# Scores, sums' transposes and the gate's sums emitted one to three ticks later in a hybrid backbone layer

## The chip, the cores and the metric

The kernel runs on one NeuronCore of a Trainium2 chip. The metric is the device time of one execution in microseconds; of several executions the median is taken. TensorE is called PE here (its weight loads PEld), VectorE DVE, ScalarE ACT, GpSimd POOL and SyncE SP.

## What is computed

One layer over 256 latent tokens and 256 context tokens, width 4096, all in float32:

```
mod_l = silu(c) @ w_ada + b_ada ;  mod_c = silu(c_ctx) @ w_ada + b_ada      # shift, scale, gate
hl = rmsnorm(xl) * (1 + sc_l) + sh_l ;  hc = rmsnorm(xc) * (1 + sc_c) + sh_c
zl = hl @ w_in ;  zc = hc @ w_in                                            # split in nine parts
ya = conformer_conv(a_val, a_glu)      # 31 taps depthwise, channel LayerNorm, swish, pointwise
yb = rg_lru forward + rg_lru backward  # short conv, two gates, one scan in each direction
yc = neighbourhood_attention(q, k, v, k_ctx, v_ctx, rpb)                    # 16 heads of 128
mix = concat(ya * silu(a_gate), yb * silu(r_gate), yc * silu(c_gate))
out = rmsnorm(xl + g_l * (mix @ w_out))
```

## The kernel before

The two big products, with `w_in` and `w_out`, are made on PE in chunks of 512 columns of weights. A chunk is cut into steps of at most two blocks of 128 rows (`kp`). For each step SP loads the raw weights (L433), ACT makes their rounded high part `hi` (L439), DVE the rest `lo` = raw - hi (L445), and `products` (L454) multiplies three times for each row block and PSUM bank: high by high, the two cross terms. A step of the later chunks has two banks, so twelve matmuls of 512 columns. `hi` and `lo` have three buffers each (`NHI`), `raw` has six (`NRAW`). During a step the program emits the `hi` and the `lo` of the step two places on.

Beside the products stand small programs written as generators ("threads"): `mod_finish` turns the sums of the modulation (`adas`) with PE transposes into columns (`psm`), `next_h`/`make_h` make the normalised input `h` from them, `attention` does four heads at a time (scores `sc` L681, softmax, transposes `pt` L706 of the probabilities `pr`, values `y`), `convs` does the 31 taps of eight channel blocks on DVE (L773, L777), `conv_ln` what follows them, and `finish` of a `GItem` sums the gate.

The gate's columns of `w_ada` are weighted and added up on DVE, 32 row blocks for each of four groups: the first block of a group starts the sum `gboth` anew (L1168), the others add to it (L1170). After the last, `finish` is spawned: eight one-column matmuls with `ones` (`psg`, L1187) sum over the partitions, and DVE adds the bias into `gcol` (L1189). The next group's first block overwrites `gboth`, so its `emit` first calls `drain` on that thread.

A tick is one group of three matmuls (of six in the chunks of the pointwise product); a step of two banks and two row blocks has four. After each group every thread that is due is advanced; `yield None` in a thread means "not before the next tick", `yield a, b` charges its time to DVE's and ACT's credit. A thread of rank 0 always goes on; the others go on only while the credit of their engine lasts. The order in which things are emitted is the order in each engine's queue. Two small functions set it, and `drain` has its own rule: it advances threads by force, without looking at the credit, and emits no products meanwhile.

```
while forced or clock[th.engine] > (clock["reserve"] if th.rank > 3 else 0):   # advance
    r = next(th.gen)                    # goes on until the thread yields None or ends
...
for t in list(threads):                                                        # drain
    if not t.done and (t in ts or t.rank == 0 or clock["aux"] > 0):
        advance(t, True)
clock["tick"] += 1
```

`clock["aux"]` counts the three small PSUM banks that are held (`take`, `give`). `convs` yields `0.5, 0` after each tap, and None only while it waits for its inputs.

Of the kernel before, what the change touches and what calls it, by code (L numbers as in the profile page):

```python
# [47 lines left out]
def tile_hybrid_layer(ctx: ExitStack, tc: tile.TileContext, x, c, cctx_tok, c_ctx, w_ada, b_ada,  # L48
# [10 lines left out]
    def page(shape, dt=F32, name="pg"):  # L59
        uid[0] += 1  # L60
        return pg.tile(shape, dt, name=f"{name}_{uid[0]}", tag="pg", bufs=NPG)
# [7 lines left out]
    def pair(name):  # L69

        if wides[0] < NWD:
            wides[0] += 1
            t = wide([P, 2, 512], name=name)
            return [t[:, 0], t[:, 1]], 1
        return [page([P, 512], name=name) for _ in range(2)], 0

    def unpair(p):
        wides[0] -= p[1]

    def bank(name, tag="aux"):  # L80


        uid[0] += 1
        return pp.tile([P, 512], F32, name=f"{name}_{uid[0]}", tag=tag, bufs=5 if tag == "g" else 3)

    def small(n, name):
        uid[0] += 1
        return sp.tile([P, n], F32, name=f"{name}_{uid[0]}", tag="small", bufs=8)
# [60 lines left out]
    def pause(n):  # L149
        for _ in range(n):  # L150
            yield None

    def take(n):

        while clock["aux"] + n > clock["limit"]:
            yield None
        clock["aux"] += n

    def give(n):
        clock["aux"] -= n  # L160

    with tc.manual_schedule():
# [49 lines left out]
        def col(name, i, n=1):  # L212
            gi, r = where[name]
            return cols[:, gi, r + i:r + i + n]
# [51 lines left out]
        def mod_columns(part, k0, s, sums):  # L266
            dst = (modG if part == 0 else modS)[:, k0:k0 + s, :]
            ba = col("b_ada", (KT if part == 0 else 0) + k0, s)[:, :, None].to_broadcast([P, s, 2])
            V.tensor_add(dst, sums[:, :s], ba)
            if part == 0:  # L270
                V.scalar_tensor_tensor(dst, dst, 1.0, col("norm_g", k0, s)[:, :, None].to_broadcast([P, s, 2]),
                                       ALU.add, ALU.mult)

        def mod_matmuls(ps, raw, k, n, W):
            for j in range(n):
                q = (k + j) % 4
                mm(ps[32 * q:32 * q + 32, :W], cpad[(k + j) // 16][:, (k + j) % 16, :], raw[:, j, :],  # L277
                   start=(k + j < 4), stop=(k + j >= KT - 4))

        def mod_finish(part, k0, s, ps):  # L280

            V.tensor_copy(adas[:, :s * P], ps[:, :s * P])
            give(1)
            yield 0.6 * s / 4 + .1, 0
            yield from pause(6)
            yield from take(1)
            pm = bank("psm")
            for i in range(s):
                tr(pm[:, i * P:(i + 1) * P], adas[:, i * P:(i + 1) * P], ident)
            yield None  # L290
            sums = small(8, "sums").rearrange("p (k o) -> p k o", o=2)
            V.reduce_sum(sums[:, :s], pm[:, :s * P].rearrange("p (k q o) -> p k o q", q=4, o=32)[:, :, 0:2], axis=AX.X)
            mod_columns(part, k0, s, sums)
            give(1)
            yield 0.5, 0
# [60 lines left out]
            V.tensor_scalar(t, t, -0.5, 1.5, ALU.mult, ALU.add)  # L356
            V.tensor_mul(y, y, t)

        for _ in range(7):
            next(fin0)  # L360
        rst = cp.tile([P, 4], F32, name="rst")
        V.reduce_sum(rst, ss, axis=AX.X)
# [273 lines left out]
        def turned(tm, i):  # L636

            ps = bank("turn")
            for j in range(2):
                for b in range(2):  # L640
                    tr(ps[:, j * T + b * P:j * T + b * P + P], tm[b][:, (i + j) * P:(i + j + 1) * P], ident)  # L641
            return ps
# [10 lines left out]
        def attention(g, st):  # L653
            qs = st["q"][0]
            yield from take(2)
            ps = [turned(qs, i) for i in (0, 2)]
            yield None
            for t, b in zip(qs, ps):
                A.copy(t.rearrange("p (r c) -> p r c", c=64)[:, :, ::-1], b.rearrange("p (r c) -> p r c", c=64))
                yield 0, 0.7  # L660
            give(2)
            q = [t[:, j * T:(j + 1) * T] for t in qs for j in range(2)]
            B, Ps = page([P, 384], name="B"), pair("pr")
            B3 = B.rearrange("p (a b) -> p a b", b=64)

            def bias(h):
                for rl in range(2):
                    G.dma_start(B3[64 * rl:64 * rl + 64],
                                bass.AP(tensor=rpb.tensor, offset=rpb.offset + h * 465 + (5 - rl) * 31 - 48,
                                        ap=[[1, 64], [31, 6], [1, 64]]))  # L670
                G.tensor_mul(B3, B3, mask[:, 0:1].to_broadcast([P, 6, 64]))
                G.tensor_add(B3, B3, mask[:, 1:2].to_broadcast([P, 6, 64]))

            for i in range(4):
                h = 4 * g + i
                bias(h)
                sums = []
                for qt in range(2):
                    yield from take(1)
                    ps = bank("sc")  # L680
                    mm(ps, q[i][:, qt * P:(qt + 1) * P], acc[("k", g), i], start=True, stop=True)  # L681
                    yield None
                    off = P * (1 - qt)
                    V.tensor_add(ps[:, T:], ps[:, T:], B[:, off:off + T])
                    nm, sm = small(1, "nm"), small(1, "sm")
                    V.reduce_max(nm, ps, axis=AX.X, negate=True)
                    yield 1.2, 0
                    A.activation(Ps[0][qt], ps, AF.Exp, bias=nm, accum_out=sm)
                    give(1)
                    yield 0, 0.7  # L690
                    sums.append(sm)
                yield None
                for qt in range(2):
                    V.reciprocal(sums[qt], sums[qt])
                    A.mul(Ps[0][qt], Ps[0][qt], sums[qt])  # L695
                    yield 0.2, 0.75
                yield None
                yield None
                yield None
                yield from take(2)  # L700
                pt = []
                for kp in range(2):
                    ps = bank("pt")
                    for kt in range(2):
                        for qt in range(2):
                            tr(ps[:, kt * T + qt * P:kt * T + qt * P + P],  # L706
                               Ps[0][qt][:, (2 * kp + kt) * P:(2 * kp + kt + 1) * P], ident)
                    pt.append(ps)
                yield None
                for kp in range(2):  # L710
                    A.copy(Ps[0][kp].rearrange("p (r c) -> p r c", c=64)[:, :, ::-1],
                           pt[kp].rearrange("p (r c) -> p r c", c=64))
                    give(1)
                    yield 0, 0.7
                yield None
                yield from take(1)
                ps = bank("y")
                for qt in range(2):
                    for kt in range(4):
                        v = acc[("v", g), kt] if kt < 2 else st["v"][0][kt - 2]  # L720
                        mm(ps[:, qt * P:(qt + 1) * P], Ps[0][kt // 2][:, (kt % 2) * T + qt * P:(kt % 2) * T + qt * P + P],  # L721
                           v[:, i * P:(i + 1) * P], start=(kt == 0 and qt == 0), stop=(kt == 3), skip_group_check=True)
                yield None
                for qt in range(2):
                    cg = st["cg"][0][qt][:, i * P:(i + 1) * P]
                    V.scalar_tensor_tensor(cg, cg, 0.5, ps[:, qt * P:(qt + 1) * P], ALU.mult, ALU.mult)
                give(1)
                yield 0.6, 0
                if i % 2:
                    yield None  # L730
                    yield from take(1)
                    ps = turned(st["cg"][0], i - 1)
                    yield None
                    split_mix([16 + h - 1, 16 + h], ps)
                    give(1)
                    yield 0.9, 0.8
            for t in (Ps, st["q"], st["v"], st["cg"]):
                unpair(t)
# [416 lines left out]
        class GItem:  # L1155
# [22 lines left out]
                return [self.emit]  # L1178

            def finish(self):  # L1180
                yield None
                yield None
                yield from take(1)
                pm = bank("psg")
                a = gboth.rearrange("p a b -> p (a b)")
                for j in range(8):
                    mm(pm[:, j:j + 1], a[:, j * P:(j + 1) * P], ones, start=True, stop=True)  # L1187
                yield None
                V.tensor_add(gcol[:, 8 * self.sg:8 * self.sg + 8], pm[:, 0:8], col("b_ada", 2 * KT + 8 * self.sg, 8))  # L1189
                give(1)  # L1190
                yield 0.1, 0
# [200 lines left out]
```

## Time and profile before

| | |
|---|---|
| median of 3 runs | 2342.5 us (2339.43 to 2342.91) |
| profiled execution, its own time | 2338.42 us |
| span from first to last instruction | 2336.6 us |
| mean granted clock of TensorE | 0.991 |
| PE busy | 2263.8 us (97%), 10761 matmuls |
| DVE, ACT busy | 1595.1 us (68%), 1251.5 us (54%) |
| read from HBM | 544.58 MB, 235 GB/s over the span |

PE is busy 97% of the span; every other engine is far below that. So the time is that of PE's queue plus PE's idle time, and a view of PE's waits says what the idle time hangs on. A matmul of 512 columns shows as 0.39 us long, but the next one starts 0.23 us after it; the starts give the pace.

### The profile page before, as it was taken

What the parts mean: (1) busy time and instruction counts of PE and PEld (TensorE: products, weight loads), DVE (VectorE), ACT (ScalarE), POOL (GpSimd) and SP (SyncE); (2) the same over time, 40 slices, a digit from 0 to 9 for tenths busy, and PEclk for the clock granted to TensorE, in tenths of its full rate; (3) what the DMA queues carried; (4) which work ended last, traced back from release to release, by engine and by line L of the source; (5) the groups of instructions that cost most, each with busy time, mean ns of one, the idle gap of its engine ahead of it and who ended that gap; (6) DMA issues with size and microseconds to landing.
All of it is one profiled execution on the core that took longest, in us unless ns stands there. A gap on an engine that the chain in (4) does not pass through costs nothing. (4 is left out here: it accounts for less than half of the span.)

```text
span 2336.6 us, 29786 instructions
## 1 busy us (share of the span) xinstructions
PE 2263.8 (97%) x10761; PEld 1748.7 (75%) x10761; DVE 1595.1 (68%) x2196; ACT 1251.5 (54%) x1846; POOL 90.6 (4%) x133
## 2 busy tenths in 40 slices
PE   6999999999999999999999999999999999999997
PEld 4556556677777888777777887888888779888886
DVE  5543477587776546676776897788777767667655
ACT  5665545465565768776754444544454544344443
POOL 0000000000000000000001000100010111000000
PEclk8999999999999999999999999999999999999999
DMA  9988888878877445555677887878887778787864
GB/s 314 290 264 281 307 270 299 293 259 258 263 258 261 132 116 156 170 171 159 168 205 212 273 283 219 225 242 261 233 217 237 184 226 306 261 266 253 262 213 162
DMA packets 293483, 550.76 MB, mean 236 GB/s; under 512 B 19199, under 2 KB 60887, under 8 KB 293335
## 3 DMA queue, kind: packets, MB, share of 16 engines
q1 hardware_dynamic: 287904, 536.94, 71.3%
q0 software_dynamic: 4480, 11.54, 4.4%
q8 instruction: 84, 1.38, 0.3%
q14 instruction: 64, 0.52, 0.1%
q10 hardware_dynamic: 951, 0.37, 0.1%
HBM read 544.58 MB, written 4.19 MB: 235 GB/s over the span
## 5 line engine op out<-in xcount | busy, mean ns | idle before, releaser
L445 DVE TENSOR_TENSOR lo<-raw,hi 128x1024 fp32r<-128x1024 f32 (+1 forms) x660 | 753.7, 1144 | 463.2 <-ACT hi L439 460.5
L439 ACT CAST hi<-raw 128x1024 fp32r<-128x1024 f32 (+1 forms) x660 | 647.4, 986 | 721.9 <-PE gtm L454 410.6
L454 PE MATMUL gtm<-hi,lh 128*128 128x512 f32 x2560 | 835.0, 401 | 1.7 <-ACT hi L439 1.7
L454 PEld LDWEIGHTS gtm<-hi,lh 128*128 128x128 f32 x2560 | 482.4, 188 | 112.5 <-issue 10.8
L454 PE MATMUL gtm<-lo,lh 128*128 128x512 f32 x1280 | 502.0, 392 | 6.4 <-DVE lo L445 6.2
L454 PE MATMUL gboth<-h,hi 128*128 128x512 f32 x1536 | 489.9, 400 | 9.1 <-ACT acc L887 3.3
L454 PEld LDWEIGHTS gboth<-h,hi 128*128 128x128 f32 x1536 | 280.3, 188 | 126.9 <-issue 52.5
L454 PE MATMUL gtm<-hi,mix 128*128 128x512 f32 x976 | 303.2, 390 | 0.0
L454 PE MATMUL gboth<-h,lo 128*128 128x512 f32 x768 | 301.2, 392 | 0.7 <-DVE lo L445 0.7
L454 PEld LDWEIGHTS gtm<-lo,lh 128*128 128x128 f32 x1280 | 241.2, 188 | 70.1 <-DVE lo L445 12.3
L454 PEld LDWEIGHTS gtm<-hi,mix 128*128 128x128 f32 x976 | 183.2, 188 | 37.9
L454 PE MATMUL gtm<-lo,mix 128*128 128x512 f32 x488 | 190.1, 390 | 0.2 <-DVE lo L445 0.2
L454 PE MATMUL gtm<-hi,h 128*128 128x512 f32 x512 | 177.7, 401 | 9.2 <-DVE acc L892 6.9
L967 DVE SCALAR_TENSOR_TENSOR gboth<-raw,scol,gboth 128x512 f32<-128x512 f32 x248 | 171.4, 746 | 0.3 <-DMA raw<-in_w_ada_dram 0.3
L454 PEld LDWEIGHTS gboth<-h,lo 128*128 128x128 f32 x768 | 144.7, 188 | 33.6 <-DVE lo L445 1.8
L887 ACT COPY acc<-gboth 128x512 f32<-128x512 f32 x216 | 123.7, 584 | 74.9 <-PE gboth L454 73.6
L1170 DVE SCALAR_TENSOR_TENSOR gboth<-raw,scol,gboth 128x1024 f32<-128x1024 f32 x124 | 160.8, 1297 | 0.0
L454 PEld LDWEIGHTS gtm<-hi,h 128*128 128x128 f32 x512 | 97.4, 190 | 43.4 <-DVE acc L892 10.0
L897 ACT COPY gboth<-acc 128x512 f32<-128x512 f32 x216 | 123.8, 591 | 8.9 <-DVE acc L892 7.2
L277 PE MATMUL psa<-raw,cpad 128*32 128x512 f32 (+2 forms) x1152 | 114.4, 470 | 1.6 <-DMA raw<-in_w_ada_dram 1.2
L454 PEld LDWEIGHTS gtm<-lo,mix 128*128 128x128 f32 x488 | 91.6, 188 | 19.5 <-DVE lo L445 0.8
L892 DVE TENSOR_TENSOR acc<-acc,gboth 128x512 f32<-128x512 f32 x72 | 49.3, 685 | 80.6 <-PE gboth L454 80.4
(227 smaller groups left out, 1673.1 us busy)
## 6 DMA issues: line engine op xcount, KB each, us to landing
raw<-in_w_in_dram SPq DMA_DIRECT2D x430, 512.0 KB, 4.5
raw<-in_w_ada_dram SPq DMA_DIRECT2D x384, 512.0 KB, 4.8
raw<-in_w_out_dram SPq DMA_DIRECT2D x128, 512.0 KB, 4.7
raw<-in_w_in_dram SPq DMA_DIRECT2D x100, 256.0 KB, 4.0
xp<-in_ctx_dram SPq DMA_DIRECT2D x16, 256.0 KB, 6.9
xp<-in_x_dram SPq DMA_DIRECT2D x16, 256.0 KB, 6.5
xr<-in_x_dram POOLq DMA_DIRECT2D x16, 256.0 KB, 5.1
raw<-in_w_pw_dram SPq DMA_DIRECT2D x8, 512.0 KB, 6.3
```

Of the source, the lines that this page charges most:

```text
L277: mm(ps[32 * q:32 * q + 32, :W], cpad[(k + j) // 16][:, (k + j) % 16, :], raw[:, j, :], start=(k + j < 4), stop=(k + j >= KT - 4))
L439: A.copy(self.hi[:, :n], self.raw[:, :n])
L445: V.tensor_sub(self.lo[:, :n], self.raw[:, :n], self.hi[:, :n].bitcast(F32))
L454: one = lambda o, l, r, start, stop: mm(o, l, r, start=start, stop=stop, skip_group_check=True)
L887: A.copy(acc[key, i], b)
L892: V.tensor_add(acc[key, i], acc[key, i], b)
L897: A.copy(ch.banks[i], acc[ch.name, i])
L967: V.scalar_tensor_tensor(a, self.raw[:, j], s, a, ALU.mult, ALU.add)
L1170: V.scalar_tensor_tensor(a, self.raw, s, a, ALU.mult, ALU.add)
```

## The change

Four places of the emission change. `mod_finish` pauses nine ticks between the copy of the sums and their transposes where it paused six, and holds a lock, `adas_busy`, from the copy to the transposes, so that a second `mod_finish` does not overwrite `adas`; the loop of the start that steps the first of these threads takes ten steps for seven. `attention` yields once more between the copies of the turned queries and the first scores. `finish` pauses five ticks before the gate's one-column matmuls where it paused two. Three `yield None` in `attention` become `pause(3)`, which is the same. No instruction is added or taken away.

```diff
+        adas_busy = []
+
         def mod_finish(part, k0, s, ps):
 
+            while adas_busy:
+                yield None
+            adas_busy.append(1)
             V.tensor_copy(adas[:, :s * P], ps[:, :s * P])
             give(1)
             yield 0.6 * s / 4 + .1, 0
-            yield from pause(6)
+            yield from pause(9)
             yield from take(1)
             pm = bank("psm")
             for i in range(s):
                 tr(pm[:, i * P:(i + 1) * P], adas[:, i * P:(i + 1) * P], ident)
+            adas_busy.clear()
             yield None
...
-        for _ in range(7):
+        for _ in range(10):
             next(fin0)
...
                 yield 0, 0.7
             give(2)
+            yield None
             q = [t[:, j * T:(j + 1) * T] for t in qs for j in range(2)]
...
-                yield None
-                yield None
-                yield None
+                yield from pause(3)
                 yield from take(2)
...
             def finish(self):
-                yield None
-                yield None
+                yield from pause(5)
                 yield from take(1)
                 pm = bank("psg")
```

The line numbers of the changed kernel are higher: L445 becomes L451, L454 L460, L289 L294, L777 L782, L1168 L1173, L1170 L1175, L1187 L1191, L1189 L1193.

Where the first gate group ends, DVE's queue before reads as follows (`gboth` is the sum, `gcol` its result, `lo` the low part of a step's weights, `conv` the taps):

```order
L777 SCALAR_TENSOR_TENSOR conv_10636<-conv_10636,cols 128x248
L1170 SCALAR_TENSOR_TENSOR gboth<-raw_11400,scol,gboth 128x1024
L445 TENSOR_TENSOR lo_11500<-raw_11402,hi_11491 128x1024
L1189 TENSOR_TENSOR gcol<-psg_11505,cols 128x8
L1168 TENSOR_SCALAR gboth<-raw_11423,scol 128x1024
L445 TENSOR_TENSOR lo_11529<-raw_11425,hi_11520 128x1024
L777 SCALAR_TENSOR_TENSOR conv_10636<-conv_10636,cols 128x249
```

Here two small operations stand between the low part of one step and that of the next. The same place of DVE's queue in the changed kernel, first and last rows:

```order
L1175 SCALAR_TENSOR_TENSOR gboth<-raw_11400,scol,gboth 128x1024
L451 TENSOR_TENSOR lo_11500<-raw_11402,hi_11491 128x1024
L782 SCALAR_TENSOR_TENSOR conv_10636<-conv_10636,cols 128x249
L782 SCALAR_TENSOR_TENSOR conv_10636<-conv_10636,cols 128x250
L782 SCALAR_TENSOR_TENSOR conv_10636<-conv_10636,cols 128x251
...
L782 SCALAR_TENSOR_TENSOR conv_10636<-conv_10637,cols,conv_10636 128x242
L782 SCALAR_TENSOR_TENSOR conv_10636<-conv_10637,cols,conv_10636 128x241
L1193 TENSOR_TENSOR gcol<-psg_11515,cols 128x8
L1173 TENSOR_SCALAR gboth<-raw_11423,scol 128x1024
L451 TENSOR_TENSOR lo_11582<-raw_11425,hi_11510 128x1024
```

Between the same two low parts now stand 53 operations of `convs` (52 taps and one L773, here L778), then the two of the gate.

PE's queue where the transposes of one modulation's sums stand (the place of about 459 us in the profile), before:

```order
L454 MATMUL gtm_3982<-hi_3947,h_715_3377 128x512
L289 MATMUL psm_4035<-ident,adas_91 128x128 x4
L454 MATMUL gtm_4042<-hi_3947,h_715_3377 128x512
L454 MATMUL gtm_4042<-lo_3962,h_715_3377 128x512
L454 MATMUL gtm_4042<-hi_3947,h_715_3377 128x512
L454 MATMUL gtm_3982<-hi_3984,h_721_3409 128x512
```

The transposes `psm` follow the first group of a step. In the changed kernel PE's queue there reads:

```order
L460 MATMUL gtm_4037<-hi_3947,h_715_3377 128x512
L460 MATMUL gtm_4037<-lo_3962,h_715_3377 128x512
L460 MATMUL gtm_4037<-hi_3947,h_715_3377 128x512
L460 MATMUL gtm_3982<-hi_3984,h_721_3409 128x512
L460 MATMUL gtm_3982<-lo_3992,h_721_3409 128x512
L460 MATMUL gtm_3982<-hi_3984,h_721_3409 128x512
L460 MATMUL gtm_3982<-hi_3984,h_731_3456 128x512
L460 MATMUL gtm_3982<-lo_3992,h_731_3456 128x512
L460 MATMUL gtm_3982<-hi_3984,h_731_3456 128x512
L294 MATMUL psm_4059<-ident,adas_91 128x128 x4
```

Nine matmuls, three groups, that stood behind the transposes now stand ahead of them.

## Rows read from the trace of the kernel before

**Rows 1.** The page, busy time of each engine.
```profile
PE 2263.8 (97%) x10761; PEld 1748.7 (75%) x10761; DVE 1595.1 (68%) x2196; ACT 1251.5 (54%) x1846; POOL 90.6 (4%) x133
```

**Rows 2.** Waits of PE: who waited for whom, us in total, times, longest.
```profile
PE gtm L454 <- DVE acc L892: 6.9, 3, 4.4
PE pt L706 <- ACT pr L695: 5.3, 6, 2.5
PE psm L289 <- DVE adas L282: 2.1, 1, 2.1
PE sc L681 <- ACT qt L659: 1.7, 1, 1.7
PE psg L1187 <- DVE gboth L1170: 0.6, 2, 0.3
```

**Rows 3.** Busy time by stretch: us; PE, PEld, DVE, ACT, POOL; clock, DMA, GB/s.
```profile
1434.00:1800.00 366.00, 366.00 (x1705) 300.36 (x1704) 290.05 (x399) 165.94 (x211) 27.99 (x33) 1.00 0.81 234
1413.88:1416.60 2.72, 2.72 (x14) 2.25 (x13) 2.57 (x5) 1.05 (x2) 0.00 (x0) 1.00 0.64 193
```

**Rows 4.** Timeline, end of the gate's first group: start, us, instruction [idle before].
```profile
1398.48 1.49 DVE L777 SCALAR_TENSOR_TENSOR conv<-conv,cols 128x243 f32<-128x243 f32 x3
...
1403.81 1.22 DVE L445 TENSOR_TENSOR lo<-raw,hi 128x1024 fp32r<-128x1024 f32 x1
...
1404.04 1.92 PE L1187 MATMUL psg<-ones,gboth 128*128 128x1 f32 x16 [0.34 <-DVE gboth L1170]
...
1406.00 0.17 DVE L1189 TENSOR_TENSOR gcol<-psg,cols 128x8 f32<-128x8 f32 x1 [0.96 <-PE psg L1187]
1406.08 0.75 DVE L1168 TENSOR_SCALAR gboth<-raw,scol 128x1024 f32<-128x1024 f32 x1
...
1413.88 0.39 PE L454 MATMUL gtm<-lo,lh 128*128 128x512 f32 x1
```

**Rows 5.** Groups of DVE by line: busy us, mean ns of one.
```profile
L777 DVE SCALAR_TENSOR_TENSOR conv<-conv,cols 128x241 f32<-128x241 f32 (+9 forms) x180 | 85.4, 475 | 3.2
```

**Rows 6.** Three short stretches, busy time and granted clock; columns as rows 3.
```profile
296.10:300.90 4.80, 4.80 (x13) 3.01 (x17) 3.36 (x6) 3.31 (x7) 0.00 (x0) 0.50 0.65 183
461.40:464.80 3.40, 3.36 (x10) 2.88 (x11) 3.40 (x6) 2.32 (x4) 0.00 (x0) 0.51 0.62 201
1406.80:1410.30 3.50, 3.50 (x10) 2.72 (x9) 1.65 (x3) 1.04 (x1) 0.00 (x0) 0.51 0.88 293
```

**Rows 7.** Timeline of PE, transposes of a modulation's sums, 459 us.
```profile
458.92 0.39 PE L454 MATMUL gtm<-hi,h 128*128 128x512 f32 x1
461.44 1.11 PE L289 MATMUL psm<-ident,adas 128*128 128x128 f32 x4 [2.13 <-DVE adas L282]
```

**Rows 8.** Timeline of PE, first scores of the last four heads.
```profile
1832.54 0.40 PE L454 MATMUL gtm<-hi,lh 128*128 128x512 f32 x1
1834.62 1.13 PE L681 MATMUL sc<-acc,qt 128*128 128x512 f32 x2 [1.68 <-ACT qt L659]
```

**Rows 9.** Timeline of DVE at 293 to 296 us.
```profile
293.25 0.87 DVE L390 SCALAR_TENSOR_TENSOR xp<-xp,modG,R 128x256 f32<-128x256 f32 x2
294.04 1.41 DVE L967 SCALAR_TENSOR_TENSOR gboth<-raw,scol,gboth 128x512 f32<-128x512 f32 x2
295.37 0.68 DVE L892 TENSOR_TENSOR acc<-acc,gboth 128x512 f32<-128x512 f32 x1
```

**Rows 10.** Timeline of PE there.
```profile
296.10 0.80 PE L454 MATMUL gtm<-hi,h 128*128 128x512 f32 x1 [4.38 <-DVE acc L892]
```

**Rows 11.** Timeline of PE around the second block's input `h`.
```profile
75.41 0.33 PE L289 MATMUL psm<-ident,adas 128*128 128x128 f32 x1
...
79.21 0.64 PE L277 MATMUL psa<-raw,cpad 128*32 128x256 f32 x8
...
87.09 0.63 PE L454 MATMUL gboth<-h,hi 128*128 128x512 f32 x2
```

**Rows 12.** Timeline of DVE there, the last write of that `h`.
```profile
78.86 0.88 DVE L382 SCALAR_TENSOR_TENSOR h<-xp,modS,h 128x256 fp32r<-128x256 f32 x2
```

**Rows 13.** Timeline of PE, transposes of probabilities in the last heads.
```profile
1915.56 1.73 PE L706 MATMUL pt<-ident,pr 128*128 128x128 f32 x5 [2.46 <-ACT pr L695]
```

## The prediction

> **What bounds the kernel now.** I read the page's busy times first: PE works 97% of the span and DVE 68% [rows 1], so only PE's idle time can be won, about 73 us of 2336.6. The view of PE's waits then says what the change can take away. The three waits that it aims at are small: 2.1 us for the copy of the sums before their transposes, once, 1.7 us for the turned queries, once, and 0.6 us in two waits for the gate's sum [rows 2]. Together that is 4.4 us, under 0.2% of the time, and 0.2% (4.7 us) is about what a measurement of this kernel can tell from no change. So the question is what the moves do to other queues. The busy time by stretch shows where a new wait would hurt: from 1434 to 1800 us PE is busy for all of 366.00 us [rows 3]. There is no idle time in which a loss could be made good.
>
> **The gate's sum, finish (two ticks to five).** This is the part that decides. A group's last block and the next group's first are emitted in neighbouring steps at the end of the first group, and a step has four ticks. With a pause of two the thread had emitted its matmuls and its `gcol` within them. With five it has not when the next group's first block comes, and that block calls `drain`. `drain` goes on by force, and `convs`, which is running there and yields None only between blocks for which it waits, then emits every tap that its finished inputs allow: two blocks' worth. The order shows the result: 53 operations in a row on DVE, between the low part of one step and that of the next. I found no such run at the other three ends of a group, nor anywhere else.
>
> Its price: three taps in a row take 1.49 us [rows 4], one takes 0.475 [rows 5], so one follows the other after (1.49 - 0.475) / 2 = 0.51 us, and 53 take 27.0 us. The low part ahead of them stands in the same order behind the same operations as before, and it ended at 1403.81 + 1.22 = 1405.03 us [rows 4]. The run then ends at 1432.1. The gate's two operations took from 1406.00 to 1406.83, 0.8 us [rows 4], and the next low part takes 1.22: it is ready at 1434.1 us. In the kernel before PE first used that part at 1413.88 us [rows 4]. PE has the same work ahead of it in both, so it waits there until 1434.1, and everything behind it comes **20.2 us** later. What covers the run at present is the two steps by which the low parts run ahead, 1413.88 - 1405.03 = 8.85 us; that is already in the 20.2. As bounds I take 19 to 22 us: taps between 0.475 us without a gap (25.2 in all) and 0.52 with a little more.
>
> ACT's casts stand waiting with three buffers, the loads with six, all full, so behind the stall three more low parts come at once and nothing else is late. The taps that DVE no longer has to do later free DVE, but PE does not wait for it there [rows 3].
>
> After the stall comes the clock. Where PE had been idle for 4.38 us [rows 10] it went on from 296.10 for 4.8 us at a granted clock of 0.50 (1.2 GHz, the lower of its two levels) [rows 6], which costs half of that, **2.4 us**. I take the same here; bounds are nothing and the double, 4.8, as the trace has no idle time as long as this one.
>
> The gate's matmuls themselves no longer wait 0.34 us, and the half clock that followed them for 3.5 us [rows 4, 6] may go; both lie before the stall, whose end DVE sets, so I count nothing.
>
> **The transposes of the modulation's sums (six ticks to nine).** PE waited 2.13 us once, at 459 us, and then ran 3.4 us at 0.51 of the clock [rows 6, 7]. Three groups, nine matmuls at 2.72 / 12 = 0.227 us each [rows 3], 2.0 us, now stand ahead: 0.1 us of the wait remains, and the half clock (1.7 us) goes with it. Gain **3.7 us**; bounds 0 to 3.8. What may be late instead is the input `h` that hangs on these sums. The tightest case is the second block's: its last write ends at 79.74 us and PE first reads it at 87.09, 7.35 us of cover [rows 11, 12]. In the changed order its transposes stand behind the matmuls of 79.21 us instead of at 75.41, so 4.4 us later [rows 11]. The cover holds with 3 us left, and I count nothing; without it each us of delay would be one of PE.
>
> At 293 us the later sums put one `xp` operation of 0.87 us behind the addition for which PE waits 4.38 us [rows 9, 10]. Gain **0.8 us**, bounds 0 to 0.9. The lock costs nothing as long as two of these threads don't overlap; where they would, the later copy waits off PE's path.
>
> **The scores (one tick later).** Once PE waited 1.68 us for the turned queries [rows 8]. One tick is three matmuls, 0.7 us, so 1.0 us of the wait stays: gain **0.7 us**, bounds 0 to 1.7. The three other groups of heads show no such wait. `pause(3)` and the ten steps at the start change nothing.
>
> **What the shifts bring besides.** With DVE free of taps after the stall, the second group of four heads goes through faster. Groups of heads without taps beside them make PE wait for the probabilities, the longest time 2.46 us [rows 13]; six such waits add up to 5.3 us [rows 2]. I take **+1.5 us**; bounds 0 and 2.46 plus a half clock of 1.7, 4.2 us.
>
> **The sum.** 20.2 + 2.4 - 3.7 - 0.8 - 0.7 + 1.5 = +18.9 us. On the profiled execution's own time, 2338.4, that gives 2357.3 us; that execution was 4.1 us faster than the median of the runs, 2342.5, on which it gives 2361.4. I forecast the middle, **2359 us**, 0.7% slower.
>
> **The rivals.** First, *PE makes the stall good*: it ends on the other side. For it speaks that the weight loads fill 300.36 of 366.00 us [rows 3], so 65.6 us are free in that stretch alone; if PE, with every input ready, could go faster than it does, it would win back the 22.6 us of stall and clock, and only the gains would be left: 2338.4 - 5.2 = 2333.2 us, faster. It decides from the point where PE's pace was set by its inputs rather than by itself. Against it speaks a step in which PE waited for nothing: twelve matmuls in 2.72 us, and the full 366 us run at that pace [rows 3]. I give it 5%. The Trainium skill, Perfetto Trace Analysis, section Identifying the Most-Contended Engine, says that TensorE's busy time is a poor measure of how near it is to its limit and that the busy share of the weight loads is the better one; by that rule 82% there would mean room to catch up, and the sum would be that of this rival.
>
> Second, *the cover is larger than it looks*: the run of taps starts well before 1405 us, or PE comes to that step later, and most of the 27 us hides. It would need some 16 us more cover than 8.85. DVE had no idle time from 1398.48 to 1405.03 but for fractions, and the order ahead is the same, so I give it 3%; the time would be about 2342 us, within 0.2%.
>
> Third, *the moves cost more*: heads without taps wait for their probabilities two or three times each with the half clock behind, or `h` is late in the early blocks, 5 to 10 us on top, 2364 to 2370 us, 12%.
>
> That the change does not do what it says can be put aside for the order, which shows the moves, but not for the waits: if the three aimed-at waits come back elsewhere the gains of 5.2 us are lost, and the time is 2362 to 2366, within the range.
>
> **How the numbers follow.** The forecast has 80%, the rivals 5, 3 and 12. Low end: the profiled execution's time with a stall of 19, a half clock of 0, all gains (6.4) and nothing new, +12.6, is 2351. High end: the median with 22, 4.8, no gains and nothing new, +26.8, is 2369; I close the range at **2351 to 2368**, which leaves out the first two rivals and the tail of the third. Faster by over 0.2%: 5%, the first rival. Within 0.2%: 3%, the second. Slower: 92%.
>
> **What would show it.** Right: one idle time of PE of some 20 us near 1410 us, ended by DVE's low part (now L451), with 53 taps without a gap on DVE in it, then a few us at half clock; the wait of 459 us gone with its half clock; that of the scores down to about 1 us; DVE's busy time the same. Wrong: no PE wait over 5 us there, or PE at a pace under 0.227 us for a matmul after it; the second block's `h` waited for; or waits for `pr` that add up to over 10 us.

## The result

The changed kernel takes 2360.43 us (median of four runs, 2358.69 to 2362.66) against 2340.97 us for the kernel before (2337.86 to 2342.91): ratio 1.0085, 95% interval 1.0069 to 1.0101. It is slower by 0.85%. The forecast was 2359 us, in a range of 2351 to 2368. The profiled execution took 2359.45 us, its span is 2357.7 us, 21.1 more than before.

The busy times on the page of the changed kernel stand beside [rows 1]: the work of every engine is the same to within 3 us, only PE's share of the span has gone down.

```profile
PE 2263.8 (96%) x10761; PEld 1746.1 (74%) x10761; DVE 1596.0 (68%) x2196; ACT 1251.6 (53%) x1846; POOL 91.9 (4%) x133
```

PE's waits in the changed kernel (who waited for whom, us in total, times, longest), to be held beside [rows 2]:

```profile
PE gtm L460 <- DVE lo L451: 29.6, 13, 22.1
...
PE pt L711 <- ACT pr L702: 6.8, 11, 2.6
...
PE gtm L460 <- DVE acc L897: 3.9, 4, 1.8
PE gtm L460 <- ACT acc L892: 3.5, 3, 1.7
...
PE gtm L460 <- ACT hi L445: 3.3, 5, 1.3
```

The three waits at which the change aims (`psm`, `sc`, `psg`) are not in this list any more. In their place stands one wait of 22.1 us for a low part. Its place is the end of the gate's first group, the place of [rows 4]. The timeline there (start, us, instruction, idle time ahead of it) shows DVE's low part, the taps, the gate's two operations and the next low part, and PE standing:

```profile
1397.71 1.22 DVE L451 TENSOR_TENSOR lo<-raw,hi 128x1024 fp32r<-128x1024 f32 x1
...
1398.85 0.99 DVE L782 SCALAR_TENSOR_TENSOR conv<-conv,cols 128x249 f32<-128x249 f32 x2
...
1424.97 0.98 DVE L782 SCALAR_TENSOR_TENSOR conv<-conv,cols,conv 128x242 f32<-128x242 f32 x2
1425.86 0.16 DVE L1193 TENSOR_TENSOR gcol<-psg,cols 128x8 f32<-128x8 f32 x1
1425.94 0.75 DVE L1173 TENSOR_SCALAR gboth<-raw,scol 128x1024 f32<-128x1024 f32 x1
1426.60 3.49 DVE L451 TENSOR_TENSOR lo<-raw,hi 128x1024 fp32r<-128x1024 f32 x3
...
1427.87 0.79 PE L460 MATMUL gtm<-lo,lh 128*128 128x512 f32 x1 [22.09 <-DVE lo L451]
```

From the end of the first low part (1397.71 + 1.22 = 1398.93) to PE's first use of the next there are 28.94 us. After the gap PE runs at half clock for 3.83 us, then at the pace of [rows 3]. Windows (us; PE, PEld, DVE, ACT, POOL busy; clock, DMA, GB/s):

```profile
1427.87:1431.70 3.83, 3.83 (x9) 3.06 (x10) 3.41 (x3) 0.00 (x0) 0.00 (x0) 0.50 0.96 299
1431.70:1434.42 2.72, 2.72 (x13) 2.21 (x13) 0.88 (x1) 1.05 (x1) 0.00 (x0) 1.00 0.94 342
1442.71:1790.00 347.29, 347.00 (x1622) 284.32 (x1621) 265.16 (x354) 158.95 (x204) 27.17 (x29) 1.00 0.80 232
```

PE has the same 8568 product matmuls in the same order in all kernels of this study, so a trace can be cut at the same matmuls and the lengths compared. Between the starts of the 1st, 1301st, 4881st, 4991st and 6831st product and the end of the span, us, before and after:

| stretch | what lies in it | before | after | difference |
|---|---|---|---|---|
| 1 to 1301 | start, modulation's sums | 428.9 | 424.2 | -4.7 |
| 1301 to 4881 | | 919.3 | 918.2 | -1.1 |
| 4881 to 4991 | end of the gate's first group | 28.9 | 50.9 | +22.0 |
| 4991 to 6831 | last taps, last four heads | 496.9 | 502.6 | +5.7 |
| 6831 to the end of the span | | 412.9 | 412.4 | -0.5 |

With 0.3 us less ahead of the first product that is the 21.1 us (the rows add up to 21.4). The third row is the stall that was forecast; the first and the fourth need the experiments.

### The profile page after: what moved, and what is told of

Read it like the earlier page. It is cut to its first block, busy times and chain, and to the rows that moved or that the text cites. A ratio compares the mean times of both kernels' runs of the same rounds, so it can differ in the third digit from the quotient of the medians.

```text
span 2357.7 us, 29802 instructions
## 1 busy us (share of the span) xinstructions
PE 2263.8 (96%) x10761; PEld 1746.1 (74%) x10761; DVE 1596.0 (68%) x2196; ACT 1251.6 (53%) x1846; POOL 91.9 (4%) x133
## 5 line engine op out<-in xcount | busy, mean ns | idle before, releaser
L451 DVE TENSOR_TENSOR lo<-raw,hi 128x1024 fp32r<-128x1024 f32 (+1 forms) x660 | 753.3, 1144 | 475.7 <-ACT hi L445 470.4
L445 ACT CAST hi<-raw 128x1024 fp32r<-128x1024 f32 (+1 forms) x660 | 647.1, 986 | 698.7 <-PE gtm L460 423.5
L460 PE MATMUL gtm<-hi,lh 128*128 128x512 f32 x2560 | 836.5, 401 | 3.3 <-ACT hi L445 3.3
L460 PEld LDWEIGHTS gtm<-hi,lh 128*128 128x128 f32 x2560 | 483.2, 189 | 114.3 <-issue 10.8
L460 PE MATMUL gtm<-lo,lh 128*128 128x512 f32 x1280 | 503.3, 393 | 29.9 <-DVE lo L451 29.4
L460 PE MATMUL gboth<-h,hi 128*128 128x512 f32 x1536 | 489.8, 400 | 9.9 <-ACT gboth L902 3.4
L460 PEld LDWEIGHTS gboth<-h,hi 128*128 128x128 f32 x1536 | 280.0, 188 | 128.9 <-issue 55.1
L460 PEld LDWEIGHTS gtm<-lo,lh 128*128 128x128 f32 x1280 | 241.9, 189 | 95.6 <-DVE lo L451 37.9
L460 PE MATMUL gtm<-hi,mix 128*128 128x512 f32 x976 | 303.0, 390 | 0.0
L460 PE MATMUL gboth<-h,lo 128*128 128x512 f32 x768 | 301.0, 392 | 0.6 <-DVE lo L451 0.6
L460 PEld LDWEIGHTS gtm<-hi,mix 128*128 128x128 f32 x976 | 183.2, 188 | 37.7
L460 PE MATMUL gtm<-lo,mix 128*128 128x512 f32 x488 | 190.1, 390 | 0.2 <-DVE lo L451 0.2
L460 PE MATMUL gtm<-hi,h 128*128 128x512 f32 x512 | 177.1, 399 | 7.4 <-DVE acc L897 3.9
L460 PEld LDWEIGHTS gboth<-h,lo 128*128 128x128 f32 x768 | 144.6, 188 | 33.5 <-DVE lo L451 1.7
L1175 DVE SCALAR_TENSOR_TENSOR gboth<-raw,scol,gboth 128x1024 f32<-128x1024 f32 x124 | 159.3, 1284 | 0.0
L460 PEld LDWEIGHTS gtm<-hi,h 128*128 128x128 f32 x512 | 96.1, 188 | 42.3 <-issue 9.0
L460 PEld LDWEIGHTS gtm<-lo,mix 128*128 128x128 f32 x488 | 91.6, 188 | 19.6 <-DVE lo L451 0.8
L460 PE MATMUL gtm<-lo,h 128*128 128x512 f32 x256 | 99.9, 390 | 0.0
```

The lines of the kernel that those rows point to most:

```text
L445: A.copy(self.hi[:, :n], self.raw[:, :n])
L451: V.tensor_sub(self.lo[:, :n], self.raw[:, :n], self.hi[:, :n].bitcast(F32))
L460: one = lambda o, l, r, start, stop: mm(o, l, r, start=start, stop=stop, skip_group_check=True)
L1175: V.scalar_tensor_tensor(a, self.raw, s, a, ALU.mult, ALU.add)
```

## The experiments

Ratios are against the kernel before, run on the same chip in the same set; a gain or loss in us is that ratio times its median there (2340.7 us in 1 to 4, 2341.4 in 5 to 8, 2342.0 in 9 to 12). The ratio is not quite that of the two medians: by the medians alone the gains of 1, 5 and 7 are 2.8, 3.7 and 3.9 us, 1.0 to 1.6 more than given below.

**1. The gate's transposes back at two ticks**, the rest of the change kept:

```diff
-                yield from pause(5)
+                yield None
+                yield None
```

> The changed kernel with `finish` back at its two ticks, so that no run of taps is forced between two `lo` at 1406 us; the later transposes of the modulation's sums and the later scores stay. Theory A (the forced run of 53 taps is the stall): the wait of `gtm` for `lo` at 1406 us, 22.09 us in the changed kernel, is back at about 2 us, the half clock after it is as before, and the gains of the two other moves are left: 2335 to 2338 us, ratio 0.997 to 0.999 against the kernel before. Rival (the stall comes from the modulation's or the scores' moves): still near 2360 us, ratio 1.008.

Measured: 2337.84 us, ratio 0.9992 (0.9981 to 1.0002). The stall is gone, the longest wait of PE for a low part is 1.3 us, and its wait for the gate's sum is back:

```profile
PE gtm L460 <- DVE lo L451: 6.2, 10, 1.3
...
1397.85 1.92 PE L1192 MATMUL psg<-ones,gboth 128*128 128x1 f32 x16 [0.34 <-DVE gboth L1175]
```

So the two other moves cannot have made the stall. What they gain, 1.9 us, lies within what the comparison can tell from nothing.

**2. That move alone**, on the kernel before (`finish` with `pause(5)`).

> The kernel before with the gate's transposes alone moved (`finish` pauses five ticks). Theory A: the whole stall of 20 to 22 us at 1406 us and none of the gains, 2362 to 2366 us, ratio 1.009 to 1.011. Rival (stall only together with the other moves): 2339 to 2343 us, ratio 1.000.

Measured: 2361.4 us, ratio 1.0094 (1.0073 to 1.0115). PE's wait is that of the changed kernel:

```profile
PE gtm L454 <- DVE lo L445: 31.5, 13, 22.1
```

The move of the gate's transposes makes the whole loss by itself.

**3. The move without the taps.** The changed kernel, but while `drain` drives generators to their end, `convs` may emit no tap; it yields None instead (`drain` sets the room to nothing at its start and to 1000 at its end, and `convs` asks for room ahead of each tap):

```diff
+        clock["room"] = 0
...
+                clock["room"] = 1000
...
+    def room():
+        while clock["room"] <= 0:
+            yield None
+        clock["room"] -= 1
...
+                    yield from room()
```

> The changed kernel, its `finish` pausing five ticks too, but the tap planner emits no tap while the gate's generators are driven to their end. Theory A (the ticks cost nothing by themselves, only the taps that they pull onto VectorE do): no wait of over 3 us at 1406 us, 2334 to 2338 us, ratio 0.997 to 0.999, as with two ticks. Rival (the later transposes hold up the gate's own values and so the next products): 2345 to 2360 us, with a wait for `gboth` or `psg` in place of that for `lo`.

Measured: 2332.64 us, ratio 0.9968 (0.9957 to 0.9979): faster than both kernels, and a little faster than expected. No wait for a low part is over 1.3 us:

```profile
PE gtm L467 <- DVE lo L458: 6.2, 10, 1.3
```

The later transposes are harmless; what `drain` lets through besides was the loss.

**4 and 8. Some of the taps.** The same with room for 26 and for 10 taps in a drain.

> As the last one, but the drain may emit 26 taps in place of 53. Theory A (each forced tap beyond the cover delays the next `lo` by its 0.5 us): the gap of TensorE at 1406 us falls from 22.1 us by 27 x 0.51 = 13.8 us to 8 to 9 us, 2342 to 2349 us, ratio 1.001 to 1.004. Rival 1 (a threshold: 26 taps are still covered): as with none, 2334 to 2338 us. Rival 2 (the stall doesn't go by the number of taps): still near 2360 us.

> As the third and fourth experiment, with 10 taps let through in the drain. With a gap of 22.09 us for 53 and 8.60 us for 26, one tap is 0.50 us, and 10 taps leave 8.60 - 16 x 0.50 = 0.6 us or less: a gap of 0 to 0.7 us at 1406 us, 2333 to 2338 us, ratio 0.997 to 0.999. Rival (the gap doesn't go in a straight line, a part of it is fixed): 2 to 4 us of it are left.

Measured with 26: 2345.6 us, ratio 1.0022 (1.0010 to 1.0033). With 10: 2334.27 us, ratio 0.9970 (0.9958 to 0.9982). PE's first use of the low part behind the taps, with 26:

```profile
1418.77 0.80 PE L467 MATMUL gtm<-lo,lh 128*128 128x512 f32 x1 [8.60 <-DVE lo L458]
```

and with 10:

```profile
1404.71 0.50 PE L467 MATMUL gtm<-lo,lh 128*128 128x512 f32 x1 [0.51 <-DVE lo L458]
```

The gap is 0.51, 8.60 and 22.09 us for 10, 26 and 53 operations: (8.60 - 0.51) / 16 = 0.51 and (22.09 - 8.60) / 27 = 0.50 us for each. It is a straight line with the price of one operation as its slope, and it meets zero at 9. So some 9 x 0.5 = 4.5 us are covered and no more. That agrees with the prediction's own rows: of the 8.85 us of cover, the gate's two operations and the low part itself take 2.0, and PE comes 2.15 us earlier where it neither waits for the gate's sum nor runs at half clock behind it (experiment 7); 4.7 us are left.

**5. The modulation's sums alone** (`mod_finish` with nine ticks, the lock, the ten steps).

> The kernel before with the change of `mod_finish` alone (nine ticks, the lock, ten steps at the start). By the prediction's two terms (3.7 us at 459 us, 0.8 us at 293 us): 4.5 us less, 2336 us, ratio 0.998. Rival (the wait for the sums goes, but waits for `acc` and `lo` of about the same size come within the next 10 us, as in the changed kernel's trace): 2339 to 2342 us, ratio 0.9993 to 1.0005.

Measured: 2337.77 us, ratio 0.9991 (0.9981 to 1.0000), 2.1 us less by the ratio, between the two. The wait of [rows 7] is gone in the trace, and a smaller one follows that the trace of the kernel before does not show:

```profile
459.04 0.60 PE L294 MATMUL psm<-ident,adas 128*128 128x128 f32 x4
471.92 0.73 PE L460 MATMUL gboth<-h,hi 128*128 128x512 f32 x2 [0.66 <-ACT gboth L903]
```

This wait of 0.64 to 0.69 us at 470 us stands in every trace with this move; of the four without it two show one of 0.3 us at that place and two none. How little one trace says here is shown by the first stretch (1st to 1301st product) in all fourteen traces: 422.5 to 430.7 us, mean 425.6, in the ten with this move, and 423.9 to 431.4, mean 428.5, in the four without it. The means differ by 2.9 us, the single traces of either kind by nearly three times that.

**6. The scores alone** (one more tick).

> The kernel before with the one more tick ahead of the scores alone. By the prediction: 1.0 of the 1.68 us of the wait for `qt` stays, 0.7 us gained, ratio 0.9997. Rival 1: the wait goes altogether, 1.7 us, ratio 0.9993. Rival 2: the later scores make the probabilities late and PE waits longer for `pr`, 1 to 4 us more, ratio 1.0005 to 1.0015. The time can hardly tell these apart; the waits of PE for `qt` and for `pr` between 1800 and 1923 us are to be read.

Measured: 2340.28 us, ratio 1.0000 (0.9990 to 1.0009). PE doesn't wait for the queries at all in this trace. The wait for the probabilities is about that of [rows 13]:

```profile
1915.97 0.33 PE L707 MATMUL pt<-ident,pr 128*128 128x128 f32 x1 [2.65 <-ACT pr L696]
```

Rival 1 by the trace; the time cannot show 1.7 us. But the wait changes with the rest of the kernel: with this tick it is nothing in 1, 1.0 us in 3 and 8 and 2.3 us in 4, without it nothing in 2, 0.7 us in 5 and 1.7 us in 7. What the tick is worth by itself stays open; it is too small for the times.

**7. The gate's transposes alone, without the taps.**

> The kernel before with the gate's transposes alone moved (five ticks), and no tap emitted while the generators are driven to their end. Theory B (the 0.3% that the third experiment gained come from the gate's later matmuls, whose wait of 0.34 us and half clock at 1407 us go): 2 to 5 us less than before, 2336 to 2339 us, ratio 0.998 to 0.999. Rival (they come from the modulation's and the scores' moves): 2340 to 2342 us, ratio 0.9995 to 1.0005.

Measured: 2337.58 us, ratio 0.9988 (0.9979 to 0.9997), 2.8 us less. The 110 products from the 4881st, in the kernel before:

```profile
1397.87:1426.80 28.93, 28.59 (x128) 23.53 (x127) 23.09 (x33) 10.09 (x10) 0.00 (x0) 0.94 0.74 237
```

and here, without the wait of 0.34 us and without the half clock of [rows 6]:

```profile
1398.30:1425.08 26.78, 26.78 (x128) 22.44 (x127) 23.00 (x33) 10.09 (x10) 0.00 (x0) 1.00 0.80 256
```

28.93 - 26.78 = 2.15 us. That is what the move of the gate's transposes has to give at the end of the first group. At the end of the fourth group, the place of the second of the two waits of [rows 2], it gives something too. There PE waits about 0.2 us in all four kernels with two ticks. In the kernel before no half clock follows, in 1, 5 and 6 it does; with five ticks there is neither. The same stretch behind the gate's matmuls in the kernel before and in 6:

```profile
2243.20:2246.80 3.60, 3.60 (x22) 3.05 (x22) 1.39 (x2) 2.02 (x3) 0.00 (x0) 1.00 0.85 307
```

```profile
2242.40:2246.00 3.60, 3.60 (x14) 3.10 (x14) 1.30 (x2) 2.03 (x3) 0.00 (x0) 0.53 0.88 324
```

From the 6831st product to the end it is 412.9 us in the kernel before, 414.5 in 1, 5 and 6 and 412.4 to 412.5 in the ten kernels with five ticks. So 0.5 to 2.1 us come on top of the 2.15, 2.7 to 4.2 in all; the 2.8 measured agree with that.

**9 to 12. The loss of the last heads.** In the changed kernel the last tap comes 105 products earlier (at the 6314th instead of the 6419th), and the last four heads lie closer: from the first transposes of their probabilities to the last there are 120 products, 219 before. At the first scores of these heads the trace shows a wait that I had not thought of. POOL loads the heads' bias `B` into a page; DVE stands at the addition of the bias to the scores, with the next step's low part behind it, and ACT at the exponential behind that, with `hi` behind it:

```profile
1848.47 0.69 DVE L842 SCALAR_TENSOR_TENSOR conv<-sq,conv 128x512 f32<-128x512 f32 x1
...
1849.92 1.32 POOL L675 DMA_DIRECT2D B<-in_rpb_dram  x2 [92.22 <-ACT sil L654]
...
1861.30 1.01 POOL L679 TENSOR_TENSOR B<-B,mask 128x384 f32<-128x384 f32 x1
...
1862.34 0.43 DVE L691 TENSOR_TENSOR sc<-sc,B 128x256 f32<-128x256 f32 x1 [5.58 <-POOL B L679]
...
1865.30 0.50 PE L460 MATMUL gtm<-hi,lh 128*128 128x512 f32 x1 [1.34 <-ACT hi L445]
1866.95 0.51 PE L460 MATMUL gtm<-lo,lh 128*128 128x512 f32 x1 [1.15 <-DVE lo L451]
```

POOL had been idle for 92 us. A page is one of 69 equal buffers (`NPG`) that many kinds of tiles use in turn, and the one that `B` gets here had held a `sq` of `conv_ln`. The profile puts POOL's wait down to ACT's `sil`, but the last reader of that `sq` is DVE's operation in the first row. It ended at 1849.16 us, 0.76 ahead of the load; the same 0.76 us lie between the two in 2, 4 and 9, where the profile names `sil`, `sh` and `sil`. In the kernel before, this bias got a page that PE's `y` had read last, and was loaded over 90 us earlier:

```profile
1757.13 1.32 POOL L668 DMA_DIRECT2D B<-in_rpb_dram  x2 [15.66 <-PE y L721]
```

In the changed kernel 12.4 us pass from the issue of the transfer to POOL's last operation on it. Theory C is that this page costs most of the 5.7 us. The test gives the bias a buffer of its own; a page has to go for it, so experiment 11 has 68 pages and nothing else, the first pair of lines here; in it every engine's operations stand in the same order as in the changed kernel:

```diff
-NPG, NWD, NRAW, NHI = 69, 6, 6, 3
+NPG, NWD, NRAW, NHI = 68, 6, 6, 3
...
+        biases = cp.tile([P, 384], F32, name="biases")
-            B, Ps = page([P, 384], name="B"), pair("pr")
+            B, Ps = biases, pair("pr")
```

> The changed kernel itself, on the same chip and against the same runs of the kernel before as the three others of this set: 2358 to 2363 us, ratio 1.008 to 1.009. Theory C and its rival expect the same of it.

> The changed kernel with a buffer of its own for the heads' bias `B`, in place of a page of the rotation (69 pages become 68, so that it fits). Theory C (of the 5 us that the last heads lose in the changed kernel, the part at 1864 us is DVE standing at the scores' addition for a bias that POOL could not load before 1849.92 us, because its page was held by `sil`; `hi` and `lo` stand behind it): POOL loads the first of these biases right after the group before, DVE's wait of 5.58 us goes, PE's waits of 1.34 and 1.15 us and the half clock behind them (1.7 us) too: 4 us less than the changed kernel, 2355 to 2358 us, ratio 1.0065 to 1.0075. Rival (the next wait, that for the probabilities, takes it up): 2359 to 2362 us, with PE's wait for `pr` longer by 2 to 4 us.

> The changed kernel with 68 pages in place of 69 and nothing else, the control of the last one. Theory C: the bias takes another page of the rotation, which may be free earlier or not; where POOL still waits for `sil` or later, 2358 to 2363 us as the changed kernel. Rival (one page fewer makes pages scarce): 2362 us or more, with waits of over 1 us for pages elsewhere.

> The eighth experiment (10 taps at most in the drain) with the bias in a buffer of its own. Theory C: in that order the last heads lie apart and POOL's bias holds up DVE only once, at the last head, without PE waiting for `lo`, so the buffer brings little: 2332 to 2336 us, ratio 0.996 to 0.998. Rival (the bias costs there too): 2 to 4 us less, 2329 to 2332 us.

Measured: the changed kernel again 2358.71 us, ratio 1.0073 (1.0062 to 1.0085). With a buffer for the bias 2352.63 us, 1.0046 (1.0034 to 1.0058). With 68 pages alone 2371.89 us, 1.0129 (1.0116 to 1.0143). With 10 taps and the buffer 2333.59 us, 0.9967 (0.9954 to 0.9979).

With its own buffer POOL loads the bias over 80 us earlier and DVE does not wait:

```profile
1768.04 1.32 POOL L677 DMA_DIRECT2D biases<-in_rpb_dram  x2 [7.86 <-DVE nm L695]
```

```profile
1859.73 0.43 DVE L693 TENSOR_TENSOR sc<-sc,biases 128x256 f32<-128x256 f32 x1
```

With 68 pages the bias takes another page, which comes free later still, and PE stands for 6.91 us:

```profile
1862.81 1.02 PE L688 MATMUL sc<-acc,qt 128*128 128x512 f32 x2
...
1864.55 1.32 POOL L675 DMA_DIRECT2D B<-in_rpb_dram  x2 [101.59 <-issue]
...
1873.26 0.43 DVE L691 TENSOR_TENSOR sc<-sc,B 128x256 f32<-128x256 f32 x1 [11.18 <-POOL B L679]
...
1876.22 0.80 PE L460 MATMUL gtm<-hi,lh 128*128 128x512 f32 x1 [6.91 <-ACT hi L445]
```

The stretch from the 4991st to the 6831st product goes with DVE's wait for the first of these biases:

| kernel | DVE's wait, us | stretch, us |
|---|---|---|
| changed, own buffer (10) | none | 494.8 |
| changed | 5.6 | 502.6 |
| changed, again (9) | 5.6 | 500.3 |
| gate's transposes alone (2) | 6.9 | 502.9 |
| 26 taps (4) | 1.2 | 498.4 |
| changed, 68 pages (11) | 11.2 | 510.9 |
| before | none | 496.9 |

The last row is of a kernel whose heads lie apart; the seven others of that order (1, 3, 5 to 8, 12) have 496.0 to 499.6 us.

Theory C holds and was put too low: the buffer took 6.1 us off the changed kernel where 4 were expected, since PE's later wait for the probabilities (2.55 and 1.50 us in the two traces of the changed kernel) went as well. The half clock that was counted is not behind the waits of 1.34 and 1.15 us, where the granted clock is 1.00, but behind that later one of 2.55, in one of the two traces. Theory C's time for the control (2358 to 2363 us) was missed; by its number the control fell to the rival, 2362 us or more. But 8 to 11 of its 13 us lie in this stretch and go with the same wait, at another page. That page had held keys (`acc`) that the scores of this very head read. The last of these matmuls is the first row above: it ended at 1863.83 us, 0.72 ahead of the load. So the bias could not be loaded before the scores to which it is added were made. Where the other 3 to 5 us of the control lie stays open; the first stretch differs by as much between traces of one kind. Held against the control, which has 68 pages too, the buffer is worth 19 us. In the order with 10 taps the heads lie apart, and the buffer changes nothing that can be measured (0.9967 against 0.9970), as theory C had it.

## Why the prediction was right, and where its terms were off

**The stall: right.** 27.0 + 0.8 + 1.22 = 29.0 us from one low part to the next was the price; the trace has 28.94. Against the kernel before, the low part ahead of the taps ended 6.1 us earlier (1398.93 against 1405.03), and PE's matmul with the next one began 14.0 us later (1427.87 against 1413.88): a step of 20.1 us, where 20.2 was forecast. PE's own wait is longer, 22.09 us, since without the gate's wait and half clock PE comes to that place 2.15 us sooner. Experiments 1 to 4 and 8 show its cause: the number of operations that `drain` lets through, at 0.50 to 0.51 us each.

**The clock: right.** 3.83 us at a granted clock of 0.50 (1.2 GHz) cost 1.9 us; 2.4 was the term, taken from a shorter idle time [rows 10]. The term lies within what the five traces with this gap show. Held against the pace of the kernel before, the 40 products after it cost 1.7 us (10), 1.9 (changed, 11), 2.2 (2) and 3.0 (9). In 9, the changed kernel again, the half clock lasts longer:

```profile
1425.94:1432.00 6.06, 6.06 (x14) 4.78 (x15) 3.41 (x3) 0.97 (x1) 0.00 (x0) 0.50 0.95 323
```

A gap five times as long did not cost clearly more.

**The wait for the gate's sum.** It was counted at nothing because the end of the stall is set by DVE. That held at the end of the first group in the changed kernel. It also hid the larger gain of this move, 2.15 us, which experiment 7 shows once the stall is away. The second of the two waits lies behind the stall, at the end of the fourth group, and was left out without a reason; the 0.5 us less in the last row of the table of stretches are its part.

**The modulation's sums: probably too high.** The terms were 3.7 and 0.8 us. The wait of 2.13 us went, but alone the move brings 2.1 us (0 to 4.4 by its interval, with the forecast of 4.5 just outside; 3.7 by the medians). The weak step is to take the 2.13 us of [rows 7] as a fixed wait of the kernel: in the three other traces without the move it is 0.8, 1.8 and 3.0 us, the half clock of 3.4 us follows it in one of these three, and where the move took it away, 0.66 us come back 12 us later. The wait for `acc` of [rows 10], at which the second term aims, became shorter by somewhat more than thought: 1.7 to 2.5 us in the ten traces with the move, 2.7 to 4.4 in the four without it. That the changed kernel's trace shows 4.7 us less in the first stretch, near the forecast, is luck in good part.

**The scores.** 0.7 us was the term. In the changed kernel the whole wait of 1.68 us went [rows 8], but it is gone in 2 as well, which has the same order of heads and not the tick, and in others with the tick part of it stayed; the times show 0 with an interval of 2 us to either side, which leaves the term open.

**What the shifts bring besides: wrong in size and cause.** The term was 1.5 us, with 4.2 as its upper end, for waits for the probabilities in heads without taps beside them. Together with the scores' gain the stretch was to lose 0.8 us; it lost 5.7 in one trace of the changed kernel and 3.4 in the other. The heads do lie closer, as thought, but the loss is not theirs: with the bias in its own buffer the same order takes 494.8 us, less than the 496.9 before. What I overlooked is that a move in the order also moves which page each tile gets, and so when POOL may start. The view that would have led there is that of DVE's and POOL's waits around `B`, which I did not read.

**The sum** came out partly by luck, since the terms missed in both directions: the gains ahead of the stall probably smaller over many runs than forecast, the late loss 2.6 to 4.9 us larger. Stall and clock, which decide, were right to 0.6 us, smaller in one trace of the changed kernel and larger in the other (22.0 and 23.1 us for the stretch, 22.6 forecast).

**The rivals.** That PE makes the stall good is refuted: in the 347.29 us after it PE is busy for 347.00 at the old pace, with the weight loads at 284.32, or 82%. The Trainium skill, Perfetto Trace Analysis, section Identifying the Most-Contended Engine, judges TensorE's headroom by its share of peak work and by the busy share of the weight loads; the second of these, 82%, misled here, since all inputs stood ready and PE did not go faster. That the cover is larger is refuted by the straight line, which starts at 9 taps. The third, further losses of 5 to 10 us in the heads, was the nearest to what happened: a part of it did happen, but it began at a page and reached the probabilities only behind that.

## What to carry to other kernels

Where a scheduler has a way to force a thread to its end, look at what else it emits on that way: a pause that is too long for its place let 53 operations through (1.0085). To bound the bystanders (0.9968) was better than to take back the pause (0.9992), since the longer pause has a gain of its own. A delay on an in-order engine can be reckoned from three rows, the number of operations, the distance of two starts and the cover, to a few tenths of a microsecond. After a change of order, look also at buffers that are used again by other tiles: a small tile that another engine must fill early is worth a buffer of its own where it would get one that comes free late (6.1 us off the changed kernel, nothing measurable in the order with 10 taps). And where an engine waited for several others, compare when each of them ended: here the profile's name for the releaser was not the right one.

## What the runs showed of the hardware

- The gate's one-column matmuls (eight in the kernel, sixteen in the trace), where they began after a wait of 0.34 us, were followed by about 3.5 us of half clock in four kernels (before, 1, 5, 6). Where they came without a wait (3, 7, 8, 12) there was none. The whole stretch differs by 2.15 us where no taps are let through (before against 7), of which only 0.34 is the wait. At the fourth group's end a wait of about 0.2 us was followed by half clock in three kernels (1, 5, 6), and in one not (before).
- An idle time of 22.09 us was followed by 3.83 us at half clock in one trace and by 6.06 in another of the same kernel, one of 8.60 (4) by 5.5, one of 4.38 by 4.8 [rows 6, 10]: the length varies from trace to trace and did not grow with the gap.
- One page fewer of 69, with every engine's operations unchanged in order, cost 13 us (2371.89 against 2358.71). By the traces 8 to 11 us of it lie in the last heads' stretch, behind a single transfer that began 8 to 9 us later, counted from that stretch's start.
